# The feed-forward's plan: other engines begin ahead of TensorE's first product, and the forms and the norm wait for the last sum into x

## The chip, the cores and the metric

The kernel runs on one core of a Trainium2 chip. The metric is the time of one execution on the device in microseconds (us). The engines are TensorE (PE, with its weight loads shown apart as PEld), VectorE (DVE), ScalarE (ACT), GpSimd (POOL) and SyncE (SP), which only issues transfers here. Every engine takes its own instructions in order and waits for the others by semaphores.

## The reference

The reference is a two-layer encoder trunk for 512 positions of width 1024, in float32. Each layer adds three things to `x`: a mixer (attention in layer 0, a chunked recurrence in layer 1), a cross-attention to a memory of 256 rows, and a gated feed-forward with a short causal convolution. The change touches the feed-forward alone, which runs once in each layer:

```
def conv_ffn(xn, w_up, conv_w, conv_b, w_down):
    h = causal_depthwise_conv(xn @ w_up, conv_w) + conv_b
    g, u = jnp.split(h, 2, axis=-1)
    return (jax.nn.gelu(g) * u) @ w_down

x = x + conv_ffn(rms_norm(x, ffn_norm[layer]), ffn_w_up[layer], ffn_conv_w[layer],
                 ffn_conv_b[layer], ffn_w_down[layer])
```

`w_up` is 1024 by 5632 and `w_down` 2816 by 1024. A final norm of `x` ends the program.

## The kernel before

**Tiles.** `x` is held transposed, as eight tiles of 128 features by 512 positions. A float32 product is made from three products of rounded parts: each operand is split into a high part (a cast on ACT) and a low part (value minus high part, on DVE), and `mm3` (L289 to L291) multiplies high by high, high by low and low by high into one accumulator. A weight block of 128 by 1024 thus costs a transfer by SP, a cast on ACT (`wh`) and a subtraction on DVE (`wl`) before PE can use it.

**The feed-forward** (`ffn_steps`) goes through 22 pairs of column blocks of `w_up`, one block of `g` and one of `u` in each pair. The first five pairs are `plain` (from L1311): two blocks of eight row steps each, then DVE takes the sums from PSUM, times the norm's factor `rb` (L1321), into a tile `hs`. Pairs 5 to 20, and 21 in layer 1, are `seven` (pair 21 of layer 0 is plain again): they form the 2 by 2 block product of a pair with seven half-size products instead of eight, in Strassen's manner (Winograd's form). For this the kernel prepares sums of the weight blocks (`s2`, `s4`, and `sa`, which a transfer by POOL accumulates in place, L1340; DVE adds `sb` from `sa` at L1362 and L1368), and sums of the halves of `x`, which are the same for all pairs: the four `forms` (ACT scales two tiles of `x` at L1247, DVE makes four sums at L1251 to L1255, ACT casts to `th` at L1264, DVE subtracts to `tl`). The first seven-product pair, p = 5, is the first user of the forms. Its first product is copied by ACT to `v` (L1394), since the same PSUM bank is then added to by the next product.

After the products of a pair comes its `tail`: ACT begins the convolution (L1278, tile `c`), DVE adds two taps for each half (L1285), ACT applies the gelu (L1293), DVE multiplies (L1295), and the result is split into `ah` (ACT, L1299) and `al` (DVE). Between the products of a seven-product pair a `fill` puts blocks of the product with `w_down` (weights `dr`), whose results DVE adds to `x` (L512).

**The norm.** The last stage ahead of the feed-forward ends in eight sums into `x` (`xadd`, L512, and `xprep`, L485 to L492, which also makes the split `xh`, `xl` and the running sum of squares `sq`). The feed-forward multiplies with the un-normed `xh`, `xl` and applies `rb` to the result, so only the evacuations wait for the norm: PE sums `sq` over the partitions (`sums`, L1218), DVE takes the root (`root`), PE spreads it (`spread`, L452) and ACT copies it to `rb` (L456).

**The order.** `Sched` plans the feed-forward. Each piece of work is a `Task` with an engine, a duration, dependencies, a due time (`prio`, counted in PE's nominal clock) and buffers to take and to free (`raw` 3, `sa` 3, `hs` 2, `c` 1, and so on). `Sched.run` lets every engine pick, again and again, the task that could start soonest; ties go to the smaller due time. The order in which it picks is the order in which instructions are written out. The framework below it may still let a later instruction of an engine pass an earlier one that it expects to wait, so that the plan sets a precedence, and the order on an engine follows it closely but not everywhere. In the plan before, all engines start at zero, and PE's first product waits for the first weight block, which the plan has ready at 8.3 of its clock (1.74 for the transfer, 4.0 until it lands, 0.95 and 1.14 for the split, and the handovers between). The plan thus has ACT and DVE do the first form and the norm's root ahead of PE's first product.

Of the kernel before, what the change touches and what calls it, by code (L numbers as in the profile page):

```python
# [71 lines left out]
class Item:  # L72
    def __init__(self, fn, dur, deps, prio, take, free, chain, pre, after, order, load, st):
        self.fn, self.dur, self.deps, self.prio, self.st = fn, dur, list(deps), prio, st
        self.take, self.free, self.chain, self.pre, self.after = take, free, chain, pre, after
        self.order, self.load = [o for o in order if o is not None], load
        self.ready = None


class Plan:  # L80
# [11 lines left out]
    def add(self, fn, dur=0.0, deps=(), prio=None, take=(), free=(), chain=(), pre=(), after=0.0, order=(), load=(), st=None):  # L92
        it = Item(fn, dur, [d for d in deps if d is not None], len(self.items) if prio is None else prio, take, free, chain, pre, after, order, load, st)
        it.n = len(self.items)
        self.items.append(it)
        return it
# [51 lines left out]
MM = 0.216  # L148


class Task:
    def __init__(self, eng, dur, fn, deps, prio, take, free, lat):
        self.eng, self.dur, self.fn, self.prio, self.lat = eng, dur, fn, prio, lat
        self.deps = [d for d in deps if d is not None]
        self.take, self.free = take, free
        self.end = None


class Sched:
# [2 lines left out]

    def __init__(self, **res):
        self.tasks = []
        self.slots = {r: [0.0] * n for r, n in res.items()}
        self.turn = {r: 0 for r in res}

    def add(self, eng, dur, fn, deps, prio, take=(), free=(), lat=0.25):
        t = Task(eng, dur, fn, deps, prio, take, free, lat)
        t.n = len(self.tasks)  # L170
        self.tasks.append(t)
        return t
# [8 lines left out]
    def run(self):  # L181
        order = sorted(self.tasks, key=lambda t: (t.prio, t.n))
        todo = {}
        want = {r: [] for r in self.slots}
        for t in order:
            todo.setdefault(t.eng, []).append(t)
        for t in self.tasks:
            for r, _ in t.take:
                want[r].append(t)
        now = {e: 0.0 for e in todo}  # L190
        inf = float("inf")
        idle = 0.0
        while any(todo.values()):
            best = None
            for e, ts in todo.items():
                soon, pick = inf, None
                for t in ts[:120]:
                    at = 0.0 if e == "-" else now[e]
                    ok = True
                    for d in t.deps:  # L200
                        if d.end is None:
                            ok = False
                            break
                        at = max(at, d.end + (0.0 if d.eng == e else d.lat))
                    if not ok:
                        continue
                    for r, _ in t.take:
                        if want[r][0] is not t:
                            ok = False
                            break  # L210
                        at = max(at, self.slots[r][self.slot(r)])
                    if not ok or at == inf:
                        continue
                    if at < soon - 1e-6:
                        soon, pick = at, t
                if pick is not None and (best is None or soon < best[0]):
                    best = (soon, e, pick)
            assert best is not None, [(e, t.n, t.prio, [d.n for d in t.deps if d.end is None], t.take) for e, ts in todo.items() for t in ts[:3]]
            at, e, t = best
            todo[e].remove(t)  # L220
            if e == "PE":
                idle += at - now[e]
            t.start, t.end = at, at + t.dur
            now[e] = t.end
            for r, st in t.take:
                want[r].pop(0)
                s = self.slot(r)
                self.turn[r] += 1
                self.slots[r][s] = inf
                st["_" + r] = s  # L230
            for r, st in t.free:
                self.slots[r][st["_" + r]] = t.end + 0.1
            if t.fn:
                t.fn()
        self.now, self.idle = now, idle


class Builder:
# [897 lines left out]
    def ffn_steps(self, layer, mp):  # L1136
# [3 lines left out]
        nc, t = self.nc, self.t  # L1140
        sc = Sched(raw=3, h=3, s2=1, s4=1, a22=1, sa=3, sb=2, ra=2, hs=2, c=1, dr=2, v=1, u2=1, u3=1, act=10, acc=4, s=2, w=2)
        add = sc.add
        tt = lambda n: 0.055 + 1.06e-3 * n
        act = lambda n: 0.1 + 0.83e-3 * n
        ACV, STT = 0.71, 0.66
# [6 lines left out]
        def pe(dur, fn, deps, take=(), free=()):  # L1152
            clock[0] += dur
            return add("PE", dur, fn, deps, clock[0] - dur, take, free, 0.2)

        def joined(deps, prio, free):
            return add("-", 0.0, None, deps, prio, (), free, 0.0)
# [3 lines left out]
        def raw_tile(st, tag):  # L1161
            pool, n, bufs = RAWS[tag]
            st[tag] = self.til(pool, tag, (P, n), bufs=bufs)
            return st[tag]
# [24 lines left out]
        def block(src, nk, xs, at, bank, deps, steps, tag="raw"):  # L1189
# [14 lines left out]
                last = pe(0.65 * per, fn, [lo, last, *deps], [(bank, st)] if c == 0 else (), [("h", st)] if c == steps - 1 else ())  # L1204
            return st, last

        own = lambda k: (self.xh[k][:], self.xl[k][:])


        def norm():  # L1210
            prev = self.state
            st = {}
            n = {}

            def sums():
                n["ps"] = self.bank("s")
                for i in range(4):
                    nc.tensor.matmul(n["ps"][:, 2 * i : 2 * i + 2], prev["sq"][:, i * P : (i + 1) * P], self.ones2[:], start=True, stop=True)  # L1218

            def root():  # L1220
                self.r = self.rsqrt(n["ps"], 4, 1.0 / DM, EPS)

            def spread():
                self.rb = self.bcast_cols(self.r, SEQ, self.sp, "rb", 1)

            a = pe(0.5, sums, (), [("s", st)])
            b = add("DVE", 2.1, root, [a], a.prio, (), [("s", st)])
            s2 = {}
            c = pe(0.5, spread, [b], [("s", s2)], [("s", s2)])
            return add("ACT", 0.52, None, [c], c.prio)  # L1230
# [9 lines left out]
        def forms(k, at):  # L1240

            st = {}

            def scaled(j):
                if j == 0:
                    st["t"] = hs2[st["_hs"]][:, :, 2:514]
                nc.scalar.activation(st["t"][:, j, :512], self.x[k + 4 * j][:], AF.Identity, scale=self.col("ffn", layer * 8 + k + 4 * j))  # L1247

            def first():
                st["r"] = raw_tile(st, "sa")[:]  # L1250
                tt_(out=st["r"][:, T1], in0=st["t"][:, 0, 0:256], in1=st["t"][:, 0, 256:512], op=ALU.subtract)  # L1251
                tt_(out=st["r"][:, T3], in0=st["t"][:, 1, 256:512], in1=st["t"][:, 0, 256:512], op=ALU.subtract)

            def second(to, a, b):
                nc.vector.scalar_tensor_tensor(out=st["r"][:, to], in0=st["r"][:, a], scalar=-1.0, in1=st["t"][:, 1, b], op0=ALU.mult, op1=ALU.subtract)  # L1255

            T1, T3, T2, T4 = (slice(256 * i, 256 * i + 256) for i in range(4))
            tt_ = nc.vector.tensor_tensor
            a = add("ACT", ACV, lambda: scaled(0), (), at, [("hs", st)])
            a = add("ACT", ACV, lambda: scaled(1), [a], at)  # L1260
            a = add("DVE", 2 * tt(256), first, [a], at, [("sa", st)])
            a = add("DVE", 0.4, lambda: second(T2, T1, slice(256, 512)), [a], at)
            a = add("DVE", 0.4, lambda: second(T4, T2, slice(0, 256)), [a], at, (), [("hs", st)])
            h = add("ACT", act(1024), lambda: nc.scalar.copy(th[k][:], st["r"]), [a], at)  # L1264
            formed.append(add("DVE", tt(1024), lambda: self.sub(tl[k][:], st["r"], th[k][:]), [h], at, (), [("sa", st)]))
# [185 lines left out]
        for p in range(22):  # L1451
            if p in due:
                queue += [(due[p], m) for m in range(8)]
            if p == 19:
                queue, late = queue[:-4], queue[-4:]
            (seven if p in SEVEN[layer] else plain)(p, fill if p >= 5 else lambda: None)
            if p < 2:
                for k in (2 * p, 2 * p + 1):
                    forms(k, clock[0] + 4.0 * (k % 2))
# [3 lines left out]
        if layer == 0:  # L1463
            for m in range(8):
                e = down(4, m, 2)
                a = add("ACT", 1.2, lambda m=m: self.xprep(m, "mix", 1, state), [e], clock[0] + 3.0)
# [369 lines left out]
```

## Time and profile before

| | us |
|---|---|
| three runs, median (lowest to highest) | 1456.62 (1454.38 to 1457.17) |
| the profiled execution | 1456.26 |
| its span, first to last instruction | 1454.5 |
| feed-forward of layer 0, PE's first product | 404.6 |
| feed-forward of layer 1, PE's first product | 1105.6 |

The profile's page gives the busy time of each engine, the chain of work that ended last, and the costliest groups of instructions. The views that are used below are of four kinds. A list of waits names who waited for whom, with the total, the times and the longest. A table by stretches gives for each stretch of the span the busy time and count for each engine, the granted clock of PE (1.00 is full speed) and the share of the DMA engines in use. A timeline has start, duration, engine, line, operation, output and inputs; a bracket at its end tells how long the engine stood idle before and what ended that. A stage is counted from PE's first product in it.

### The profile page before, as it was taken

The numbers are of one execution on the slowest core, as the hardware profiler recorded it, in microseconds if no ns is written. First come the engines' busy times: TensorE is split into PE (matmuls) and PEld (weight loads), VectorE is DVE, ScalarE is ACT, GpSimd is POOL, SyncE is SP. The second block draws the span as 40 slices with busy tenths as digits, with TensorE's granted clock in tenths as the row PEclk, the third lists the DMA queues.
The fourth block names the chain that finished last, engine by engine and source line by source line (L and its number), as shares of the span: only waits on it lengthen the run. The fifth ranks groups of instructions, "written<-read, shape, count | busy, mean of one in ns | idle before, by whom it ended". The sixth has DMA issues, their size and how long they took to land.

```text
span 1454.5 us, 22322 instructions
## 1 busy us (share of the span) xinstructions
PE 1423.8 (98%) x8366; PEld 1269.8 (87%) x8366; DVE 1177.4 (81%) x2206; ACT 826.3 (57%) x1416; POOL 58.7 (4%) x101
## 2 busy tenths in 40 slices
PE   9999999999998999999999999999999989999998
PEld 7888868899887999999888788889988889999997
DVE  7778886766687999999778868676667889999985
ACT  7767574444464566666456734445445556666654
POOL 0000120000000000000000100000000000000000
PEclk9999999999999999999999999999999999999999
DMA  5222314323236566652232232323323656666412
GB/s 200 88 73 73 102 32 158 117 86 131 87 123 180 150 167 159 169 156 77 84 102 87 73 102 80 109 93 125 116 87 123 174 153 153 174 154 167 124 59 80
DMA packets 61213, 172.55 MB, mean 119 GB/s; under 512 B 6704, under 2 KB 6704, under 8 KB 61104
## 3 DMA queue, kind: packets, MB, share of 16 engines
q1 hardware_dynamic: 55344, 152.69, 31.9%
q0 software_dynamic: 4752, 17.30, 7.0%
q8 instruction: 66, 1.08, 0.3%
q10 hardware_dynamic: 1008, 1.12, 0.2%
q14 instruction: 43, 0.35, 0.1%
HBM read 168.99 MB, written 2.10 MB: 118 GB/s over the span
## 4 chain that ended last, share of the span: by engine, by line
PE 78%; DVE 13%; ACT 4%; issue 3%; DMA 2%; POOL 0%; SPq 0%; DVEq 0%; ACTq 0%; POOLq 0%
PE acc L289 15%; PE acc L291 14%; PE acc L290 14%; PE w L289 5%; PE w L290 5%; PE w L291 5%; DVE wl L279 3%; PE s L289 2%; PE s L290 2%; PE s L291 2%; PE acc L351 2%; PE acc L352 2%; PE acc L353 2%; DVE c L1285 2%; DMA sa<-in_up_dram 1%
## 5 line engine op out<-in xcount | busy, mean ns | idle before, releaser
L289 PE MATMUL acc<-xh,wh 128*128 128x512 f32 (+1 forms) x824 | 289.2, 351 | 0.0
L291 PE MATMUL acc<-xh,wl 128*128 128x512 f32 (+1 forms) x824 | 285.0, 346 | 0.0
L290 PE MATMUL acc<-xl,wh 128*128 128x512 f32 (+1 forms) x824 | 284.8, 346 | 0.0
L279 DVE TENSOR_TENSOR wl<-raw,wh 128x1024 fp32r<-128x1024 f32 (+2 forms) x200 | 239.3, 1196 | 38.2 <-ACT wh L282 35.7
L282 ACT CAST wh<-raw 128x1024 fp32r<-128x1024 f32 (+2 forms) x137 | 140.3, 1026 | 155.2 <-PE acc L290 95.8
L291 PEld LDWEIGHTS acc<-xh,wl 128*128 128x128 f32 x824 | 156.5, 190 | 14.8
L289 PEld LDWEIGHTS acc<-xh,wh 128*128 128x128 f32 x824 | 156.6, 190 | 14.3
L290 PEld LDWEIGHTS acc<-xl,wh 128*128 128x128 f32 x824 | 156.7, 190 | 14.2
L1285 DVE SCALAR_TENSOR_TENSOR c<-hs,vec,c 128x512 f32<-128x512 f32 x176 | 129.2, 746 | 2.7 <-ACT c L1278 2.6
L289 PE MATMUL w<-ah,wh 128*128 128x512 f32 x304 | 115.7, 381 | 0.0
L290 PE MATMUL w<-al,wh 128*128 128x512 f32 x304 | 115.5, 380 | 0.0
L291 PE MATMUL w<-ah,wl 128*128 128x512 f32 x304 | 115.3, 379 | 0.0
L1278 ACT ACTIVATE c<-hs,vec 128x512 f32<-128x512 f32 x88 | 67.5, 809 | 19.1 <-DVE hs L1422 9.3
L291 PEld LDWEIGHTS w<-ah,wl 128*128 128x128 f32 x304 | 57.6, 189 | 8.2
L289 PEld LDWEIGHTS w<-ah,wh 128*128 128x128 f32 x304 | 58.0, 191 | 6.7
L290 PEld LDWEIGHTS w<-al,wh 128*128 128x128 f32 x304 | 57.9, 190 | 6.6
L289 PE MATMUL acc<-mem,wh 128*128 128x256 f32 (+1 forms) x192 | 60.3, 314 | 0.0
L291 PE MATMUL acc<-mem,wl 128*128 128x256 f32 (+1 forms) x192 | 59.7, 311 | 0.0
L1299 ACT CAST ah<-c 128x512 fp32r<-128x512 f32 x44 | 27.2, 619 | 57.0 <-DVE c L1295 56.9
L290 PE MATMUL acc<-mem,wh 128*128 128x256 f32 (+1 forms) x192 | 59.6, 310 | 0.0
L512 DVE TENSOR_TENSOR x<-w,x 128x512 f32<-128x512 f32 x72 | 49.4, 686 | 7.9 <-PE w L291 7.7
L512 DVE TENSOR_TENSOR x<-acc,x 128x512 f32<-128x512 f32 x32 | 22.0, 690 | 40.4 <-PE acc L291 40.4
(373 smaller groups left out, 3810.3 us busy)
## 6 DMA issues: line engine op xcount, KB each, us to landing
raw<-in_up_dram SPq DMA_DIRECT2D x55, 512.0 KB, 3.2
sa<-in_up_dram SPq DMA_DIRECT2D x33, 512.0 KB, 4.2
sa<-in_up_dram POOLq DMA_DIRECT2D x33, 512.0 KB, 5.5
dr<-in_down_dram SPq DMA_DIRECT2D x64, 256.0 KB, 3.6
ra<-in_up_dram SPq DMA_DIRECT2D x33, 256.0 KB, 3.3
raw<-in_xk_dram SPq DMA_DIRECT2D x16, 512.0 KB, 3.2
raw<-in_wo_dram SPq DMA_DIRECT2D x16, 512.0 KB, 3.2
raw<-in_xq_dram SPq DMA_DIRECT2D x16, 512.0 KB, 3.3
```

The lines of the kernel that those rows point to most:

```text
L279: self.nc.vector.tensor_tensor(out=lo, in0=v, in1=hi.bitcast(F32), op=ALU.subtract)
L282: self.nc.scalar.copy(hi, v)
L289: mm(out, wh, xh, start=first, stop=False, skip_group_check=parts)
L290: mm(out, wh, xl, start=False, stop=False, skip_group_check=parts)
L291: mm(out, wl, xh, start=False, stop=last, skip_group_check=parts)
L351: mm(ps, xh[k][:, ts], wh, start=(k == 0), stop=False)
L352: mm(ps, xh[k][:, ts], wl, start=False, stop=False)
L353: mm(ps, xl[k][:, ts], wh, start=False, stop=(k == 7))
L512: self.nc.vector.tensor_tensor(out=x, in0=restored(ps[:]), in1=x, op=ALU.add)
L1278: nc.scalar.activation(st["c_"][:, j, :], hs()[:, j, 2:514], AF.Identity, scale=self.col("cw", (layer * 3 + 2) * 44 + blk), bias=self.col( ...
L1285: nc.vector.scalar_tensor_tensor(out=c, in0=hs()[:, j, n : n + 512], scalar=w, in1=c, op0=ALU.mult, op1=ALU.add)
L1299: nc.scalar.copy(acts[p][0][:], u())
```

## The change

`AHEAD` gives each engine but PE a start ahead of zero: SP by 14, POOL by 10, ACT and DVE by 5. Buffers are free from −14. PE still starts at zero, so the plan can have weights ready by then. `Task` gets a field `after`, before which it can't be planned. The first scaling of each form is barred until 0.8 and the norm's `sums` until 3.4, and three tasks without a function take 0.6 (DVE, from 0.2), 1.2 (ACT, from 1.0) and 1.3 (DVE, from 1.8) of the plan's time: they stand for the last `xadd` and `xprep` of the stage before. No instruction is added or removed, and no dependency on the chip is altered; what can differ is the order in which instructions are written out.

```
+AHEAD = {"SP": 14.0, "POOL": 10.0, "ACT": 5.0, "DVE": 5.0}
...
 class Sched:
...
-        self.slots = {r: [0.0] * n for r, n in res.items()}
+        self.slots = {r: [-AHEAD["SP"]] * n for r, n in res.items()}
...
-    def add(self, eng, dur, fn, deps, prio, take=(), free=(), lat=0.25):
-        t = Task(eng, dur, fn, deps, prio, take, free, lat)
+    def add(self, eng, dur, fn, deps, prio, take=(), free=(), lat=0.25, after=-99.0):
+        t = Task(eng, dur, fn, deps, prio, take, free, lat, after)
...
-        now = {e: 0.0 for e in todo}
+        now = {e: -AHEAD.get(e, 0.0) for e in todo}
...
-                    at = 0.0 if e == "-" else now[e]
+                    at = max(t.after, -99.0 if e == "-" else now[e])
...
+        X_LAST = 0.8
+        add("DVE", 0.6, None, (), -20.0, after=0.2)
+        add("ACT", 1.2, None, (), -20.0, after=1.0)
+        add("DVE", 1.3, None, (), -20.0, after=1.8)
...
             a = pe(0.5, sums, (), [("s", st)])
+            a.after = 3.4
...
-            a = add("ACT", ACV, lambda: scaled(0), (), at, [("hs", st)])
+            a = add("ACT", ACV, lambda: scaled(0), (), at, [("hs", st)], after=X_LAST)
```

More of the change, by code (lines that the diff above doesn't have):

```diff
@@ L148, with __init__ @@
 MM = 0.216
+AHEAD = {"SP": 14.0, "POOL": 10.0, "ACT": 5.0, "DVE": 5.0}
 class Task:
-    def __init__(self, eng, dur, fn, deps, prio, take, free, lat):
+    def __init__(self, eng, dur, fn, deps, prio, take, free, lat, after):
+        self.after = after
         self.eng, self.dur, self.fn, self.prio, self.lat = eng, dur, fn, prio, lat
```

## The prediction

> **What bounds the kernel now.** I read the page's totals first, then PE's waits in stretches of the span, then the stretch with the longest wait as a timeline of each engine.
>
> ```profile
> span 1454.5 us, 22322 instructions
> PE 1423.8 (98%) x8366; PEld 1269.8 (87%) x8366; DVE 1177.4 (81%) x2206; ACT 826.3 (57%) x1416; POOL 58.7 (4%) x101
> ```
>
> PE is busy for 98% of the span. So only two things count: time in which PE waits, and time in which its clock is down. The waits of PE and of its weight loads, first from 404 to 470 us and then from 1105 to 1172 us (the heads of the two feed-forward stages; columns: total, times, longest):
>
> ```profile
> PE acc L289 <- ACT v L1394: 6.8, 1, 6.8
> PEld s L1218 <- DVE sq L486: 0.5, 1, 0.5
> PEld s L452 <- DVE sqt L446: 0.5, 1, 0.5
> ...
> PE acc L289 <- ACT v L1394: 6.3, 1, 6.3
> PEld s L1218 <- DVE sq L486: 0.5, 1, 0.5
> ```
>
> Each stage has one long wait, for the copy `v` of its first seven-product pair (p = 5, the first after five plain pairs), and two of 0.5 us at the norm. Busy time by stretch (PE, PEld, DVE, ACT, POOL, then granted clock, DMA share, GB/s):
>
> ```profile
> 417.40:446.30 28.90, 28.90 (x135) 25.32 (x134) 28.89 (x44) 21.19 (x27) 1.86 (x2) 1.00 0.46 150
> 446.30:455.00 8.70, 8.70 (x42) 7.61 (x41) 1.84 (x4) 2.17 (x3) 0.84 (x1) 1.00 1.00 225
> 461.10:468.05 6.95, 0.14 (x2) 0.00 (x0) 6.08 (x10) 3.49 (x7) 0.46 (x1) 0.78 0.38 132
> 468.05:472.00 3.95, 3.95 (x16) 3.74 (x17) 3.82 (x7) 1.99 (x4) 0.40 (x1) 0.53 0.75 151
> 1169.00:1173.00 4.00, 4.00 (x20) 3.81 (x20) 3.87 (x7) 1.60 (x4) 0.00 (x0) 0.69 0.91 179
> 480.00:760.00 280.00, 279.43 (x1914) 261.67 (x1913) 254.29 (x391) 163.15 (x266) 10.81 (x14) 1.00 0.49 133
> ```
>
> From 480 to 760 us PE loses 0.57 of 280 us, so the rest of the stage holds nothing to win. What can be won lies at the head: the waits of 6.8 and 6.3 us, and the slow clock behind them, 3.95 × (1 − 0.53) = 1.86 us and 4.00 × (1 − 0.69) = 1.24 us, 16.2 us in all. Its cause, on DVE (first two rows) and then ACT:
>
> ```profile
> 450.81 0.69 DVE L1362 TENSOR_TENSOR sb<-sa,raw 128x512 f32<-128x512 f32 x1 [4.50 <-DMA sa<-in_up_dram]
> 454.46 0.69 DVE L1362 TENSOR_TENSOR sb<-sa,raw 128x512 f32<-128x512 f32 x1 [2.35 <-DMA sa<-in_up_dram]
> ...
> 460.59 1.03 ACT L1356 CAST wh<-sa 128x1024 fp32r<-128x1024 f32 x1
> 464.31 0.62 ACT L1299 CAST ah<-c 128x512 fp32r<-128x512 f32 x1 [2.70 <-DVE c L1295]
> 465.69 0.81 ACT L1278 ACTIVATE c<-hs,vec 128x512 f32<-128x512 f32 x1 [0.76 <-DVE al L279]
> 466.41 0.60 ACT L1183 CAST wh<-dr 128x512 fp32r<-128x512 f32 x1
> 466.92 0.81 ACT L1278 ACTIVATE c<-hs,vec 128x512 f32<-128x512 f32 x1
> 467.64 0.36 ACT L1394 ACTIVATE v<-acc 128x256 f32<-128x256 f32 x1
> ```
>
> DVE had no idle time from 417.4 to 446.3 (28.89 of 28.90 busy), then stood 4.50 + 2.35 = 6.85 us in front of sums that need the accumulated `sa` tiles, and stayed that far behind. `v` itself was ready at 461, when its product had ended, but on ACT it stood behind the tails of pairs 3 and 4 (`ah`, two `c`), which waited for the late DVE.
>
> **The change part by part.** It adds no instruction on the chip (the three new tasks have no function) and removes none. It alters the order in which the feed-forward's instructions are written out. All prices are against this profiled execution: span 1454.5, whole 1456.26 us, 0.36 below the median of 1456.62.
>
> *SP 14 and POOL 10 ahead.* In the plan the three first weight loads, the two `ra` and the two `dr` move before zero. On the chip they are there already:
>
> ```profile
> 401.70 0.33 SPq L1169 DMA_DIRECT2D raw<-in_up_dram  x1
> 402.12 0.38 SPq L1169 DMA_DIRECT2D ra<-in_up_dram  x1
> ...
> 436.54 0.33 SPq L1169 DMA_DIRECT2D raw<-in_up_dram  x1
> 436.96 1.69 SPq L1169 DMA_DIRECT2D sa<-in_up_dram  x2
> 442.91 1.00 POOL L1340 DMA_DIRECT2D sa<-in_up_dram  x1 [70.58 <-PE acc L290]
> ```
>
> SP issues a `raw` whenever one of its three tiles comes free, and the first `ra` 2.2 us ahead of the stage; POOL's first accumulation waits for the `sa` load of 436.96. A start allowed sooner moves none of them: 0. The cover is the tile, not the queue. If `ra` or `dr` slipped ahead of the `raw` of 401.70, that load would lose their issue time, 0.4 us each, with 10 us to spare. The two `sa` loads follow the fourth form in the plan, and on the queue the `raw` of 436.54; neither order is altered by the start. The 446.3 to 455 row shows all 16 DMA engines full while those transfers run. The Trainium skill, "DMA: Bandwidth & Descriptors", section "Issuing engines are not separate DMA queues", says transfers begun from several engines share the same 16 and save only issue time; the trace's share of 1.00 agrees. By that rule the 6.85 us stay; were an earlier issue enough to land them in time, the sum would be that of the rival "all of it" below, and the rule takes chance from it.
>
> *ACT and DVE 5 ahead.* Three weight casts and subtractions now stand before zero. The chip does that too: PE's first product of the stage, at 404.56 (below), met its weights ready, so nothing is won by planning them sooner: 0. If they were late, PE would wait for a cast and a subtraction, 1.03 + 1.22 us by the rows of such tiles below and above.
>
> *The norm's sums not before 3.4.* The plan had them first of all, so on the chip they were let in as soon as `sq` seemed ready:
>
> ```profile
> 404.56 0.38 PE L289 MATMUL acc<-xh,wh 128*128 128x512 f32 x1
> 404.77 0.38 PE L290 MATMUL acc<-xl,wh 128*128 128x512 f32 x1
> 408.50 1.05 PE L1218 MATMUL s<-ones,sq 128*128 128x2 f32 x8
> 417.42 1.29 DVE L1321 TENSOR_TENSOR hs<-acc,rb 128x512 f32<-128x512 f32 x2 [1.31 <-ACT rb L456]
> ```
>
> PE is given its first step of the block (to 2.6 of the plan's clock), is then free with the sums still barred, takes the second step, and only then the sums: after 24 products instead of 17. Products follow at 0.215 us (404.56 to 404.77, shown rounded), so 404.56 + 24 × 0.215 = 409.7 instead of 408.50. The wait of 0.5 us for `sq` goes: −0.5 per stage, −1.0. In return `rb` and the evacuation at 417.42 come up to 1.2 us later. DVE is full from there to 446.3, so that is passed on, but 6.85 us of waiting for DMA follow it. Bounds: 0 where the wait swallows it, +1.2 per stage where the `sa` loads slip too (the `raw` ahead of them on SP waits for DVE's subtraction). I take 0 for the sum and keep +2.4 for the range.
>
> *Forms from 0.8, and the three blocks for the last `xadd` and `xprep`.* In the old plan the first form and the norm were done before PE's first product and cost nothing; in the new one the form's DVE work and the blocks of 0.6 and 1.3 stand behind it. Every later DVE task of the plain pairs moves back against PE, by 1 to 2 us as I add them up by hand. In the old plan's own clock (an order, no time of the chip) `v` stood 0.8 behind the first `c` of pair 4, so that pair of tasks changes places. So I expect `v` ahead of both `c` of pair 4, and perhaps of `ah`. On the chip `v` could then follow the cast of 460.59, at 461.62, and end at 461.98; the next product, 12 of half the width at half of 0.215, runs 1.3 us, to 463.3. What is late next is the first down block:
>
> ```profile
> 465.57 0.69 DVE L1321 TENSOR_TENSOR hs<-acc,rb 128x512 f32<-128x512 f32 x1
> 467.05 0.69 DVE L279 TENSOR_TENSOR wl<-dr,wh 128x512 fp32r<-128x512 f32 x1 [0.79 <-ACT wh L1183]
> 470.77 0.63 PE L289 MATMUL w<-ah,wh 128*128 128x512 f32 x1
> 473.87 0.27 PE L289 MATMUL s<-th,wh 128*128 128x256 f32 x1
> ```
>
> Its cast comes early, so DVE's 0.79 us of waiting goes and `wl` is done at 465.57 + 0.60 + 0.69 = 466.9. PE has then stood 3.6 us and starts slowly again. If it runs at half speed for 3.6 us (468.05 to about 471.7 in the old run), that is 8.4 products at 0.43 and 3.6 at 0.215, done at 471.3 instead of 473.87, a gain of 2.6; in the second stage, whose wait was 0.5 shorter, 2.1. Bounds: 0, if ACT keeps its order, and 16.2, if DVE's lag goes as well; below nothing, if the tails put off are missed. I take 4.7, nearest to the rows of ACT and DVE above, which show one queue's order mended and the other's lag left.
>
> Sum: −1.0 − 4.7 = −5.7, so 1456.26 − 5.7 = 1450.6.
>
> **Rivals.**
>
> *All of it.* The new order also puts DVE's two sums behind work that is ready. Then 16.2 + 1.0 = 17.2 go: 1439.1. For it: only two instructions stand wrongly. Against: nothing in the edit moves their loads.
>
> *The clock is kept.* If PE's remaining wait stays short enough, the slow stretch goes too: the down block ends at 466.9 + 12 × 0.215 = 469.5, a gain of 4.4 and 3.9, with the norm 9.3: 1447.0. The rows show 0.53 behind 6.8 us of waiting and 0.69 behind 6.3. The Trainium skill, "TensorE: Matmul & The Clock Gate", section "Why this matters for your kernels", puts the limit at idle gaps over about 3 us; the trace agrees in that both gaps lie above it, and no row here shows a shorter one. My 3.6 lies at the edge.
>
> *No change that can be measured.* ACT and DVE keep their order around 446 to 468; only the norm moves: −1.0 + (0 to 2.4), 1455.3 to 1457.7. For it: PE had no wait in the old plan either, and the stall came all the same.
>
> *Slower: DVE later.* The norm's 1.2 us and the first form's DVE work of up to 2.9 us (four pieces of 0.42 and a subtraction of 1.22, rows below) fall in the stretch in which DVE is full, and the `sa` loads slip with it: 4.1 per stage, 8.2 − 1.0 = +7.2: 1463.5. It decides as soon as the `raw` of 436.54 slips by as much as DVE does, since the DMA wait then swallows nothing.
>
> ```profile
> 408.70 0.42 DVE L1255 SCALAR_TENSOR_TENSOR sa<-sa,hs 128x256 f32<-128x256 f32 x1
> 411.22 1.22 DVE L279 TENSOR_TENSOR tl<-sa,th 128x1024 fp32r<-128x1024 f32 x1
> 441.84 2.07 DVE L1285 SCALAR_TENSOR_TENSOR c<-hs,vec,c 128x512 f32<-128x512 f32 x3
> ```
>
> *Slower: a new wait.* A tail put off keeps one of two `hs` tiles and the only `c`, which pair 5 needs. A tail is four taps of 0.69 and two more DVE steps of 0.6, 3.9 us; if PE waits for one in each stage, 7.8 − 1.0 = +6.8: 1463.1, and with a second one 1471.
>
> **How the numbers follow.** Forecast (1448 to 1453.3) 0.24; clock kept 0.07; all of it 0.15; no change 0.14; DVE later 0.22; a new wait 0.18. Faster is the first three, 0.46; slower the last two, 0.40. A measurement of this kernel can tell about 0.2%, 2.9 us. The likeliest is 1450.6, and 0.36 for the median: 1451. Cases of both signs hold the chance, so the range goes from "all of it", 1439, to DVE later with 1.5 us more, 1465; it leaves out 0.05 below and 0.12 above. The forecast's own range is 1448 to 1453.3.
>
> **What would show it.** The wait for `v` at 3.5 us or less in both stages, with `ah` or both `c` behind `v` on ACT; PE's next wait for `wl<-dr`; no wait for `sq` at L1218, which follows 24 products; `ra`, `dr` and `sa` issued where they were. Wrong if DVE meets L1362 at another place in its order, if `sa` is issued later than 33 us into the stage, or if a wait for `hs` or `c` appears after `v`.

## The result and the profile after

The changed kernel takes 1442.52 us in the median (1440.56 to 1443.46), against 1455.84 for the kernel before in the same session: a ratio of 0.9907, 95% interval 0.989 to 0.9924. It is faster by 13 us. The profiled execution took 1440.56 us.

The page of after, its span and busy times:

```profile
span 1438.8 us, 22323 instructions
PE 1419.1 (99%) x8366; PEld 1266.7 (88%) x8366; DVE 1178.0 (82%) x2206; ACT 826.8 (57%) x1416; POOL 58.7 (4%) x101
```

The waits of after, of PE and of its weight loads in the head of the first feed-forward, and of PE in that of the second (total, times, longest). The line numbers in these rows are 4 to 9 higher than before.

```profile
PE acc L293 <- ACT v L1403: 1.3, 1, 1.3
PE s L456 <- DVE sqt L450: 0.2, 1, 0.2
PEld s L456 <- DVE sqt L450: 0.9, 2, 0.6
...
PE acc L293 <- ACT v L1403: 1.1, 1, 1.1
```

The two waits for `v` are 2.4 us together instead of 13.1: 10.7 us are gone. The stretches of after (PE, PEld, DVE, ACT, POOL, granted clock, DMA share, GB/s):

```profile
416.00:446.00 30.00, 30.00 (x141) 26.27 (x140) 28.66 (x45) 20.45 (x27) 1.86 (x2) 1.00 0.58 164
460.80:465.00 4.20, 4.20 (x26) 3.88 (x27) 4.17 (x8) 2.73 (x6) 0.33 (x1) 1.00 0.81 145
1154.50:1158.50 4.00, 4.00 (x26) 3.68 (x26) 3.96 (x8) 2.75 (x6) 0.18 (x1) 1.00 0.85 160
```

Behind the shorter waits the clock stays at 1.00, where it was 0.53 and 0.69: the 3.1 us of slow clock are gone as well. 10.7 + 3.1 = 13.8 us accounts for the difference of 13.3 us between the medians. (The two profiled spans differ by 15.7; 1.65 of that lies ahead of the first feed-forward, which starts at 402.91 instead of 404.56 in code that is the same. In the trace of before PE's clock was 0.50 from 198.72 to 202.13 us, half of 3.41 us lost; in that of after it was 1.00 there. The last section says when that happens.)

Where it came from: first POOL's second accumulating copy in before, then the timelines of SP and POOL, DVE, and ACT and PE of after:

```profile
444.22 0.86 POOL L1340 DMA_DIRECT2D sa<-in_up_dram  x1 [0.31 <-DVE c L1285]
...
429.62 4.51 SPq L1173 DMA_DIRECT2D sa<-in_up_dram  x2
436.75 0.34 SPq L1173 DMA_DIRECT2D raw<-in_up_dram  x1
434.64 1.00 POOL L1349 DMA_DIRECT2D sa<-in_up_dram  x1 [63.95 <-DVE c L1294]
438.37 0.86 POOL L1349 DMA_DIRECT2D sa<-in_up_dram  x1 [2.74 <-DVE al L283]
...
445.82 0.70 DVE L1371 TENSOR_TENSOR sb<-sa,raw 128x512 f32<-128x512 f32 x1
447.17 0.69 DVE L1371 TENSOR_TENSOR sb<-sa,raw 128x512 f32<-128x512 f32 x1
...
457.03 0.62 ACT L1308 CAST ah<-c 128x512 fp32r<-128x512 f32 x1 [2.70 <-DVE c L1304]
458.41 0.81 ACT L1287 ACTIVATE c<-hs,vec 128x512 f32<-128x512 f32 x1 [0.76 <-DVE al L283]
459.63 0.81 ACT L1287 ACTIVATE c<-hs,vec 128x512 f32<-128x512 f32 x1
460.35 0.36 ACT L1403 ACTIVATE v<-acc 128x256 f32<-128x256 f32 x1
460.77 0.38 PE L293 MATMUL acc<-th,s2h 128*128 128x256 f32 x1 [1.25 <-ACT v L1403]
```

Three things are to be seen. On SP the two `sa` loads of pairs 5 and 6 now stand ahead of the plain `raw`; before, `raw` went out at 436.54 and the `sa` loads from 436.96 on. POOL's accumulating copies therefore start 31.7 and 35.5 us into the stage (434.64 and 438.37 less 402.91) instead of 38.4 and 39.7 (442.91 and 444.22 less 404.56). DVE's two sums no longer stand idle, and ACT's order around `v` is what it was: `ah` and both `c` still ahead of it.

The DMA engines in the same part of the stage, from the rows of POOL's stretches (POOL busy, granted clock, DMA share, GB/s), first before, then after:

```profile
430.00:438.00 8.00, 0.00 (x0) 1.00 0.26 79
438.00:446.00 8.00, 1.86 (x2) 1.00 0.95 323
446.00:455.00 9.00, 0.84 (x1) 1.00 1.02 225
```

```profile
430.00:438.00 8.00, 1.00 (x1) 1.00 0.74 205
438.00:446.00 8.00, 0.86 (x1) 1.00 1.01 263
446.00:455.00 9.00, 0.84 (x1) 1.00 0.77 215
```

The transfers that filled 446 to 455 had been issued late, behind eight microseconds in which the DMA engines stood three quarters idle. Issued earlier, they use those.

The order of instructions, read from the programs as they are written out, says how the swap came about; of SP's head starts that are named here only 14 was run. Both plans write the two `sa` loads ahead of that `raw`. The layer under the plan let `raw` pass them before; with SP's head start it doesn't. That is one swap in each feed-forward, and all of the difference on SP in this stretch. A head start of 6, 10, 14 or 20 for SP gives it, whatever ACT and DVE have, and with a head start of zero for SP it doesn't come. The bars and the three empty tasks alone, with no head start, give every engine the order of before, so there was nothing to measure in them. Without the bar on the norm's sums the order is that of the changed kernel.

### The profile page after: what moved, and what is told of

Read it like the earlier page. It is cut to its first block, busy times and chain, and to the rows that moved or that the text cites. A ratio compares the mean times of both kernels' runs of the same rounds, so it can differ in the third digit from the quotient of the medians.

```text
span 1438.8 us, 22323 instructions
## 1 busy us (share of the span) xinstructions
PE 1419.1 (99%) x8366; PEld 1266.7 (88%) x8366; DVE 1178.0 (82%) x2206; ACT 826.8 (57%) x1416; POOL 58.7 (4%) x101
## 4 chain that ended last, share of the span: by engine, by line
PE 79%; DVE 13%; ACT 4%; issue 3%; DMA 1%; POOL 0%; SPq 0%; DVEq 0%; ACTq 0%; POOLq 0%
PE acc L293 15%; PE acc L295 15%; PE acc L294 15%; PE w L293 5%; PE w L295 5%; PE w L294 5%; DVE wl L283 2%; PE s L293 2%; PE s L294 2%; PE s L295 2%; PE acc L355 2%; PE acc L356 2%; PE acc L357 2%; DVE c L1294 2%; PE w L1632 1%
## 5 line engine op out<-in xcount | busy, mean ns | idle before, releaser
L295 PEld LDWEIGHTS acc<-xh,wl 128*128 128x128 f32 x824 | 156.5, 190 | 14.9
L1187 ACT CAST wh<-raw 128x1024 fp32r<-128x1024 f32 (+1 forms) x30 | 29.7, 989 | 44.7 <-PE acc L294 21.0
```

The costliest lines, as they stand in the source:

```text
L295: mm(out, wl, xh, start=False, stop=last, skip_group_check=parts)
L1187: nc.scalar.copy(st["wh"][:, :cols], st[tag][:, :cols])
```

## The experiments

Theory A: the swap on SP's queue carries the change. Theory B: the changed order at the head of DVE's, ACT's and PE's queues carries it. Theory C, from the forecast: what counts is that `v` passes the tails on ACT. All runs compute the whole reference. Medians and ratios go against the kernel before in the same session (1456.0 to 1457.4 us).

| | us | ratio (95%) | waits for `v`, us |
|---|---|---|---|
| before, `sa` loads first | 1441.33 | 0.9895 (0.9881 to 0.991) | 1.0, 1.4 |
| after, `raw` first | 1460.07 | 1.0025 (1.0015 to 1.0035) | 7.2, 7.2 |
| after, SP's start alone | 1442.09 | 0.99 (0.9885 to 0.9914) | 1.1, 1.2 |
| after, the starts without the bars | 1441.0 | 0.9892 (0.9878 to 0.9905) | 2.1, 1.2 |
| before, one `sa` load first | 1451.58 | 0.9961 (0.9947 to 0.9975) | 5.9, 2.2 |
| before, `v` first | 1446.15 | 0.993 (0.9915 to 0.9945) | 0.9, 1.0 |
| after, `v` first | 1438.13 | 0.9872 (0.9858 to 0.9885) | none |
| after, `v` ahead of both `c` only | 1438.57 | 0.9876 (0.9862 to 0.9889) | none |
| before, `sa` loads and `v` first | 1438.49 | 0.9874 (0.9857 to 0.989) | none |

**The swap alone, in the kernel before.** The plain load of pair 5 is issued behind the `sa` load of pair 6; every other engine keeps its order.

```
-            l2 = load(r2, "raw", A1, 1024, at - 12.0)
+            l2 = load(r2, "raw", A1, 1024, at - 12.0, f"raw{p}", "sa6" if p == 5 else None)
...
+                if behind:
+                    with tc.issue_after(issued[behind]):
+                        issued[name] = nc.sync.dma_start(to, src).ins
```

> The kernel before, with one swap: in each feed-forward the plain load `raw` of pair 5 (L1173's DMA_DIRECT2D raw<-in_up_dram, at 436.54 us before) is issued behind the two `sa` loads of pairs 5 and 6 on SyncE's queue, as it stands in the changed kernel. The instructions of every other engine keep the order of before. Theory A (the swap on SyncE's queue carries the change): the accumulating copies of `sa` are issued some 8 and 4 us earlier, VectorE's two sums of `sa` and `sb` no longer wait for them (6.9 us and 6.3 us before), the wait for `v` falls from 6.8 and 6.3 to about 1.3 and 1.1 us, and the time is 1442 to 1446 us. Theory B (the new order at the head of VectorE's and ScalarE's queues, with the norm's sums after 24 products, carries it): the two waits for `v` stay near 6.5 us and the time is 1455 to 1458 us. Theory C, the forecast's (what counts is that `v` passes `ah` and the two `c` on ScalarE): they stay ahead of `v` here, so no more than the transfer's part can come back; 1455 to 1458 us.

It took 1441.33 us, a little under theory A's range: the swap alone gives all of the gain. Its SP and DVE timelines in the first feed-forward:

```profile
430.41 1.75 SPq L1176 DMA_DIRECT2D sa<-in_up_dram  x2
434.85 0.34 SPq L1174 DMA_DIRECT2D raw<-in_up_dram  x1
...
446.92 0.69 DVE L1369 TENSOR_TENSOR sb<-sa,raw 128x512 f32<-128x512 f32 x1 [1.10 <-DMA sa<-in_up_dram]
```

The `sa` loads go out 4.4 us ahead of that `raw`, which has to wait for DVE's `wl` to free a tile. Of DVE's 6.9 us of waiting there 1.1 is left. Theories B and C fall as causes of this change.

**The swap undone, in the changed kernel.**

```
+                if name in ("sa5", "sa6"):
+                    put_off.append((to, src))
+                    return
...
+                if name == "raw5":
+                    with tc.issue_after(issued[name]):
+                        for to, s_ in put_off:
+                            nc.sync.dma_start(to.rearrange("p (a b) -> p a b", a=2), s_)
```

> The changed kernel with the one swap undone: the two `sa` loads of pairs 5 and 6 stand behind `raw` of pair 5 on SyncE's queue again, as before the change; TensorE, VectorE, ScalarE and GpSimd keep the changed kernel's order. Theory A: the waits for `v` return to 6 to 7 us in each feed-forward, the granted clock falls behind them, and the time is 1454 to 1458 us, less the half microsecond a stage of the norm's sums (1453 to 1457). Theory B: the waits stay at 1 to 1.5 us and the time is 1441 to 1444 us. Between the two, a time near 1449 would say that each carries a half.

1460.07 us: the gain goes, and the kernel is slower than before by 0.25%, which no theory had. Its waits (PE in the first and second head, then DVE in the first):

```profile
PE acc L293 <- ACT v L1417: 7.2, 1, 7.2
PE acc L295 <- DVE wl L283: 1.2, 1, 1.2
...
PE acc L293 <- ACT v L1417: 7.2, 1, 7.2
...
DVE sb L1385 <- DMA sa<-in_up_dram: 7.4, 2, 4.9
```

The waits for `v` are 0.4 and 0.9 longer than before, and a wait of 1.2 us for `wl` is new. With the late loads, the changed order of DVE, ACT and PE thus costs 3.9 us (1456.22 to 1460.07); with the early ones it costs nothing that can be told.

**SP's start alone, and the four starts without the bars.**

```
-AHEAD = {"SP": 14.0, "POOL": 10.0, "ACT": 5.0, "DVE": 5.0}
+AHEAD = {"SP": 14.0, "POOL": 0.0, "ACT": 0.0, "DVE": 0.0}
```

> The changed kernel with SyncE's head start alone: GpSimd, ScalarE and VectorE begin the plan with TensorE's first product again; the bars on the forms and the norm stay. Theory A: SyncE's order has the swap, so 1441 to 1445 us, as the whole change. Theory B: the head of VectorE's and ScalarE's queues is that of before but for a few places, so 1452 to 1457 us. A time between would be the worth of ScalarE's and VectorE's five microseconds.

For the second run the starts are those of the change; `X_LAST`, the three empty tasks and both uses of `after` are taken out.

> The changed kernel's four head starts without the bars: the two placeholder tasks on VectorE and the one on ScalarE are gone, and the forms and the norm's sums wait for no given time. SyncE's order has the swap. Theory A: 1441 to 1444 us, as the whole change (which stood at 1442.5). If the bars carry a part of it, 1445 us and more.

1442.09 and 1441.0 us, both as the whole change. The starts of POOL, ACT and DVE, and the bars, each left out by itself, are worth nothing that these runs can tell. The first of the two does not part theory A from theory B, though. It was expected to have nearly the old order at the head of DVE's and ACT's queues; its trace has the norm's sums behind 24 products and DVE's first evacuation 13.50 us into the stage, both as in the changed kernel. What parts them are the two runs above.

**Half the swap.** In the kernel before, only the `sa` load of pair 5 goes ahead of `raw`.

```
+            l2 = load(r2, "raw", A1, 1024, at - 12.0, f"raw{p}", "sa5" if p == 5 else None)
...
+                if name in ("sa6",):
+                    put_off.append((to, src))
```

> The kernel before with half the swap: on SyncE's queue the `sa` load of pair 5 goes ahead of the plain load of pair 5, the `sa` load of pair 6 stays behind it. Theory A: VectorE's first sum of `sa` no longer waits (4.5 us before), the second still does, by 3 to 4 us, since its load goes out near 437 us and its accumulating copy some 4 us later; the waits for `v` are then 3.5 to 5 us, and the time is 1446 to 1452 us, by whether the granted clock falls behind a wait of that length. If one load carries all of it: 1441 to 1444 us, or 1455 to 1458 us.

1451.58 us, in theory A's range: a third of the gain. DVE's waits in the first and second head, then PE's:

```profile
DVE sb L1376 <- DMA sa<-in_up_dram: 6.0, 1, 6.0
...
DVE sb L1376 <- DMA sa<-in_up_dram: 2.3, 1, 2.3
...
PE acc L289 <- ACT v L1408: 5.9, 1, 5.9
...
PE acc L289 <- ACT v L1408: 2.2, 1, 2.2
```

As expected the first sum doesn't wait and the second does, but by 6.0 and 2.3 us, not 3 to 4. The two stages differ in the second `sa` load: issued at 437.07 in the first, it took 9.4 us to land, and POOL's second copy, which needs it, goes out at 447.05; in the second stage the same load took 5.3 us. Why it took longer in the first is left open. What is clear is that both loads have to be early.

**The forecast's own step, by hand.** In the kernel before, `v` of pair 5 is put ahead of `ah` of pair 3 and of both `c` of pair 4; SP keeps its order.

```
+            if p == 5:
+                for x in told["late"]:
+                    x.deps.append(v)
...
+                    with tc.issue_after(told["v"]):
+                        return fn()
```

> The kernel before, with the forecast's own step done by hand: on ScalarE `v` of pair 5 stands ahead of `ah` of pair 3 and of both `c` of pair 4; SyncE's order stays that of before, so VectorE still waits for `sa`. The forecast's step priced this at 2.6 + 2.1 = 4.7 us off the two waits for `v`: 1450 to 1453 us, with the waits at 3.5 to 4.5 us. If the place of `ah` and `c` is worth nothing, because they wait for VectorE's own late work and ScalarE would stand anyway, 1455 to 1458 us; if TensorE then stands for `hs` or for wh and wl of pair 3 instead, 1457 us and more.

1446.15 us, 10 us faster, twice the forecast's price. PE's waits in the first head, DVE's, the timeline of ACT, and PE's stretch behind the wait (PE busy, granted clock, DMA share, GB/s):

```profile
PE w L291 <- DVE wl L279: 1.6, 1, 1.6
PE acc L289 <- ACT v L1410: 0.9, 1, 0.9
PE acc L289 <- ACT u L1410: 0.9, 1, 0.9
...
DVE sb L1378 <- DMA sa<-in_up_dram: 6.5, 2, 4.0
...
460.05 0.37 ACT L1410 ACTIVATE v<-acc 128x256 f32<-128x256 f32 x1
462.32 0.62 ACT L1313 CAST ah<-c 128x512 fp32r<-128x512 f32 x1 [1.90 <-DVE c L1309]
...
464.00:468.00 4.00, 3.85 (x25) 1.00 0.75 171
```

DVE still stands 6.5 us for the transfers. But its delay reached PE through `v`: out of its place behind the tails `v` is waited for by 0.9 us, `wl` and `u`, which are late next, by 1.6 and 0.9, and in these short pieces, 3.4 us instead of 6.8, the clock stays at 1.00. So the forecast's mechanism exists and is worth 10 us; this change doesn't use it.

**Both together.** The same step in the changed kernel, once whole and once with `ah` left ahead of `v`; and in the kernel before, both hand edits with no head start.

```
-                told["late"] = [h]
+                told["late"] = []
```

> The changed kernel with `v` of pair 5 put ahead of `ah` of pair 3 and of both `c` of pair 4 on ScalarE, in both feed-forwards: the step that took 10 us off the kernel before when it was done alone there. If the two gains add up, the rest of the waits for `v` (1.3 and 1.1 us) goes and the time is 1439.5 to 1441.5 us. If the two remove the same wait, what is left is too little to pay for what comes later: `wl` of pair 3 and `u` are late by 1.6 and 0.9 us in each feed-forward, as in the run on the kernel before, and the time is 1443 to 1446 us, as that run's.

> The changed kernel with `v` of pair 5 ahead of only the two `c` of pair 4 on ScalarE; `ah` of pair 3 stays ahead of `v`. If the two `c` are what holds `v` (`ah` ends at 457.65 us, `v` starts at 460.35 us), the waits of 1.3 and 1.1 us go and nothing of pair 3 is late: 1439.5 to 1441.5 us. If the sums that wait for the two `c` come late on VectorE instead, 1442 to 1445 us.

> The kernel before with both hand edits and nothing of the head starts: on SyncE the two `sa` loads of pairs 5 and 6 ahead of the plain load of pair 5, and on ScalarE `v` of pair 5 ahead of `ah` of pair 3 and both `c` of pair 4. On the changed kernel the second edit took 4.4 us off (1442.5 to 1438.1). If the head starts and bars of the change add nothing beyond the swap on SyncE, this is as fast as that one: 1436.5 to 1439 us, and no wait for `v` is left. If the changed order at the head of VectorE's and ScalarE's queues is needed for `v` to pass, waits for `wl` or `u` remain as in the run with the second edit alone, and the time is 1440 to 1446 us.

1438.13, 1438.57 and 1438.49 us: the three are the same, in the range or a little under it, and no wait for `v` is left in any of them. PE's stretch behind `v`'s place in the first of them:

```profile
460.00:464.00 4.00, 4.00 (x28) 1.00 0.61 122
```

PE doesn't stop there at all, and the feared late `wl` and `u` aren't waited for, since DVE isn't behind any more. The interval of the first (0.9858 to 0.9885) lies below that of the change itself (0.989 to 0.9924): this is faster than both kernels, by 4 us against the changed one, of which the waits for `v` account for 2.4; the rest is not accounted for. The third shows that the two orders are all that is needed; the head starts bring nothing of their own.

**The clock by itself.** The kernel before with both edits, `v` copied several times over into the same tile, to make PE wait by a chosen length.

```
+                for _ in range(8 if p == 5 and tag == "v" else 1):
+                    done = nc.scalar.activation(folded(st[tag][:]), bank("Y")(), AF.Copy, scale=scale)
```

The other two runs had 10 and 13 in the place of the 8.

> The kernel before with both hand edits, and `v` of pair 5 copied 8 times over into the same tile instead of once, so that TensorE must wait for it again by a chosen length: seven more copies of some 0.34 us less 0.4 us of room, about 2.0 us in each feed-forward. It measures the price of the granted clock by itself. If the clock falls behind gaps of over about 3 us alone, as the forecast took it, the stretch of 4 us behind the wait stays at 1.00, and the time is 1442 to 1444 us. If it may fall behind 2.2 us, as in one stage of the half swap, 2.0 us is at the edge: 1442 to 1447 us.

> As the run with 8 copies, with 10: a wait of about 2.7 us in each feed-forward. If the limit is about 3 us: clock 1.00 behind it, 1443 to 1446 us. If it is near 2.2 us: a clock of 0.5 to 0.7 in the 4 us behind it, in both feed-forwards, and 1446 to 1450 us.

> As the run with 8 copies, with 13: a wait of about 3.7 us in each feed-forward, over either limit. The clock falls to 0.5 to 0.7 in the 4 us behind it in both feed-forwards, each costing some 1.2 to 2 us: 1448 to 1452 us.

1439.66, 1440.67 and 1443.14 us, one run each beside 1456.52 for the kernel before. They missed their aim. With 13 copies PE waits only

```profile
PE acc L289 <- ACT v L1418: 0.8, 1, 0.8
```

(0.5 and 0.6 with 8 and 10), because the order of PE changed with it and products of the first down block moved ahead of the wait. The clock stayed at 1.00 behind them, which says nothing of longer gaps. With 13 copies the time is 4.7 us over the run without them (1438.49), of which the two waits are 1.6; the rest is not explained.

## Why the prediction was right and wrong

The time of 1442.5 lies in the range, and the side was right, but the 1451 rested on a mechanism that didn't take place. The range, 1439 to 1465, held cases of both signs, and that the side came out right was luck: with SP's order put back, all else that the change does, for which the forecast had −5.7 us, took 3.9 us more than the kernel before. The time came near the rival "all of it" (1439.1, given 0.15), with 2.4 us of waiting left, but not by that rival's cause. It had DVE's two sums put behind work that is ready; what happened is that their loads came earlier, the step that the prediction put at 0.

- **What bounds the kernel: right.** The 16.2 us of waits for `v` and slow clock are what there was to win, nearly. The change took 13.8 of them; the two orders together took all waits for `v`, and 17.9 us (1456.03 to 1438.13), of which 1.7 are not explained by them.
- **"A start allowed sooner moves none of them: 0", "neither order is altered by the start", and "nothing in the edit moves their loads": wrong.** This is the step that failed, and the swap alone in the kernel before measures it at 14.9 us (1456.22 to 1441.33). In after the first `sa` load goes out 26.7 us into the stage instead of 32.4. The prediction looked at what releases each transfer by itself and took "the cover is the tile, not the queue". For the two `sa` loads it was the queue: they stood behind a `raw` that waited for its own tile, and once it had gone out the first of them had to wait only 0.9 us more. SP's waits before, from 424 to 437.3 us, show it: two plain loads that wait for DVE's `wl` to free a tile, up to 4.5 us, and the second is the one ahead of the `sa` loads:

```profile
SPq L1169 <- DVE wl L279: 8.9, 2, 4.5
```

- **The full DMA engines: misread.** The prediction took the share of 1.00 from 446 to 455 us to mean that an earlier issue gains little, and let the rule of the Trainium skill ("DMA: Bandwidth & Descriptors", "Issuing engines are not separate DMA queues") take chance from "all of it". The rule speaks of which engine issues, not of when; no run here moves a load to another engine, so it is neither borne out nor contradicted. The row that mattered was the stretch ahead, 430 to 438, with a share of 0.26.
- **"`v` ahead of both `c`": didn't happen**, in the changed kernel ACT has the old order there. The term of −4.7 was also too small where the step was done by hand: 10.1. The rival "the clock is kept" had the better working (4.4 + 3.9 = 8.3 without the norm).
- **The forms' bar and the three blocks: nothing. "DVE later": hidden.** The bars change no engine's order without the head starts, and little with them. DVE's order did change with SP's start, and where the loads stayed late it cost 3.9 us with ACT's and PE's (1460.07), of the 7.2 that "DVE later" had. With the early loads no loss shows, and DVE is a little less full than before (28.66 of 30.00 us from 416 to 446, against 28.89 of 28.90).
- **The norm: right in kind, too large in size.** PE's start of the stage and the sums, and DVE's first evacuation in after:

```profile
402.91 0.38 PE L293 MATMUL acc<-xh,wh 128*128 128x512 f32 x1
408.09 0.95 PE L1226 MATMUL s<-ones,sq 128*128 128x2 f32 x8
416.41 1.28 DVE L1330 TENSOR_TENSOR hs<-acc,rb 128x512 f32<-128x512 f32 x2
```

The sums follow 5.18 us, 24 products of 0.215, into the stage, and the wait for `sq` is gone; but the wait of the weight loads for `sqt` grew from 0.5 to 0.9, so 0.1 us is won for each stage, not 0.5. The evacuation comes 13.50 us into the stage instead of 12.86: 0.64 later, with no loss that shows. It is the head start, not the bar, that moves the sums: in the run without the bars they follow 24 products too.
- **ACT and DVE 5 ahead at 0: right** (SP's start alone 1442.09, the whole change 1442.52).

## What to carry to other kernels

When a transfer lands late, look first at the queue that issues it: what stands ahead of it there, and for which tile that one waits. A stretch with full DMA engines, as here, is no proof that bandwidth is the bound; read the share of the stretch before it. And the stall of another engine cost TensorE here only through the instructions that it waits for, above all `v`, so there are two cures, to bring the late data earlier or to take that instruction out from behind the late work, and here each alone gave 10 us or more.

## What the runs showed of the hardware

The granted clock fell behind a shorter gap than expected. In the run with half the swap, second feed-forward, PE stood 2.18 us up to 1164.21; in the run of the starts without the bars, first feed-forward, 2.09 us up to 461.37. For each, the timeline's row first, then stretches (PE busy, granted clock, DMA share, GB/s):

```profile
1164.21 0.38 PE L289 MATMUL acc<-th,s2h 128*128 128x256 f32 x1 [2.18 <-ACT v L1408]
...
1161.54:1164.95 3.41, 1.23 (x11) 1.00 0.32 123
1164.95:1168.37 3.42, 3.42 (x13) 0.50 0.99 199
```

```profile
461.37 0.38 PE L293 MATMUL acc<-th,s2h 128*128 128x256 f32 x1 [2.09 <-ACT v L1398]
...
456.91:460.33 3.42, 2.37 (x22) 1.00 0.46 153
460.33:463.74 3.41, 2.37 (x17) 1.00 0.45 73
463.74:467.15 3.41, 3.41 (x25) 1.00 0.98 232
```

The clock halved some 0.7 us after the first gap had ended and stayed so for 3.4 us; behind the second it stayed at 1.00. The traces tell the two apart. In each of them the clock changes only at times that lie whole multiples of 3.413 us apart (in before at 198.72, 202.13, 464.96, 471.78, 1164.69 and 1171.52 us, among others), and the stretches above are cut at multiples of it. The gap of 2.18 us lies in one such stretch whole, and in the next the clock is 0.50. The gap of 2.09 us is cut in two at 460.33, and either stretch has some 1.04 us of idle time.

Over the fourteen traces, every such stretch at full clock in which PE is idle for 1.75 us or more, 23 in all, is followed by one at 0.50, and none with 1.73 us or less is. The slow stretch at 198.72 in before is a case with a short gap: its longest is 1.43 us, but the stretch ahead of it has 1.76 us of idle time.

```profile
195.30:198.72 3.42, 1.66 (x9) 1.00 0.03 5
198.72:202.13 3.41, 3.41 (x7) 0.50 0.00 0
```

So what decides in these traces is not the length of one gap but PE's idle time within a fixed stretch of 3.41 us, and a gap of about 2 us costs something or nothing by where it falls. The Trainium skill, "TensorE: Matmul & The Clock Gate", "Why this matters for your kernels", sets the limit at over about 3 us; the measurement of 2.18 us speaks against it as a safe bound.
